# Two-layer trunk: causal mask by a bf16 product, softmax scaling on ScalarE, modulation chunks turned through DRAM

## The chip, the cores and the metric

The kernel runs on one core of a Trainium2 chip as one program. The metric is the time of one execution on the device in microseconds (us), median over runs. TensorE (PE in the rows) multiplies; VectorE (DVE), ScalarE (ACT) and GpSimd (POOL) work element by element; SyncE (SP) issues most of the DMAs. Each engine runs its own list of instructions in order and waits on semaphores for the others.

## The reference

512 tokens of width 1024 go through two layers. The conditioning vector c gives each layer six modulation vectors, which the kernel works out in three chunks of two (ada_w is 24 MB a layer). Layer 0 mixes tokens with 16-head attention with a forget gate, layer 1 with causal pooling; each layer ends in a mixture of 32 experts, two per token.

```
c_act = silu(c)
mod = c_act @ ada_w[i] + ada_b[i]
sh_m, sc_m, gt_m, sh_f, sc_f, gt_f = split(mod, 6)
h = rmsnorm(x, norm_mix_g[i]) * (1 + sc_m) + sh_m
# layer 0: attention, 16 heads of 64
logits = q @ k.T / 8 + F[t] - F[s]       # F = cumsum(log_sigmoid(x @ w_f + f_bias))
logits = where(s <= t, logits, -inf)
o = softmax(logits) @ v
x = x + gt_m * (o @ w_o)
h = rmsnorm(x, norm_ffn_g[i]) * (1 + sc_f) + sh_f
x = x + gt_f * experts(h)                # sigmoid router, best group of four, top 2 of 32
```

## The kernel before

**Attention.** The heads are taken in eight pairs (hp), each in four blocks of 128 queries (qt): 32 units, u = 4 hp + qt. `attention` writes the order of TensorE, VectorE and ScalarE by hand. A unit u does `flip(u)` (TensorE turns the scaled probabilities sb by products with the identity, L873; ScalarE copies them to pT, L874), then `scores(u + 1)`, then `normalise(u + 1)`, then `values(u)` (L882). `scores` makes 128 x n logits for each of the two heads in two products (L854 with the high parts of q and k, L855 with the low parts and the rows of the gate F); VectorE adds the causal mask on the last 128 columns (L856) and takes the negated maximum (L857); ScalarE takes the exponential with its sum (L858). `normalise` takes the reciprocal (L863) and multiplies the row by it on VectorE (L865).

**Projections.** Between these stand the steps of `project(hp + 1)`: 24 triples of products of 128x512 (L735) for q, k and v of the next pair. Numbers are split into a high and a low part of reduced precision, so each product is three. `close("q")` and `close("k")` take a finished sum out of PSUM: four casts on ScalarE (L771, L772 for q, L774, L775 for k) and two subtractions on VectorE (L778 for q, L781 for k). The v sum is turned by L789 and copied by VectorE (L791). `split` makes the halves of a pair's weights, the high one on ScalarE (L744), the low one on GpSimd (L745).

**Modulation.** Chunk (0, 0) is needed first: `ada_first` makes it on TensorE from eight loaded pieces. The other five chunks, 40 pieces in the list `late`, are multiplied and added up on VectorE, one piece of 128x2048 an operation (`ada_piece`, L332 and L334); the table `units` says after which unit each piece comes, EARLY pieces come before the loop. After the eighth piece TensorE sums over partitions (L342), `ada_turn` copies the row out of PSUM (L308), turns it into columns by 32 small products (L313), and `ada_close` adds the bias on VectorE (L350). The weights of everything come through one stream of slots in a fixed order. `small_loads` issues the small inputs, among them wf, the weights of the forget gates (used by `forget_gates`, L705).

**Behind the attention.** `wo_split` and `o_split` make the halves of the output weights and of the attention's result (ScalarE L919, VectorE L920); `out_ahead` and `out_step` multiply them. The router follows (L430 to L439), then the experts, whose large weight buffer can only be filled when the front's pools are closed.

## Time and profile before

| | us |
|---|---|
| median of 3 runs | 1364.91 |
| lowest and highest | 1362.5 and 1366.27 |
| the profiled execution | 1366.04 |
| its span in the trace | 1364.5 |
| mean granted TensorE clock | 0.946 |

The span is the time from the first to the last instruction of the trace; the profiled execution took 1.5 us more. In the rows below, times are microseconds from the start of the span unless marked ns. The granted clock is a share of 2.4 GHz: 0.50 is the lower of TensorE's two levels, 1.2 GHz. "[0.30 <-DVE sb L865]" says that the engine was idle for 0.30 us before the instruction and that line 865 on VectorE released it.

### The profile page before, as it was taken

The page shows a single profiled execution, that of the slowest core. Times are in us where ns is not written, and L with a number is a line of the kernel's source. Part 1 is how long each engine was busy: PE and PEld are TensorE (multiplying, and loading weights), DVE is VectorE, ACT ScalarE, POOL GpSimd, SP SyncE. Part 2 cuts the span into 40 slices and gives each one's busy share as a digit, 9 for nine tenths or more (in the row PEclk, how much of TensorE's full clock was granted, in tenths as well). Part 3 has the DMA queues.
Part 4 walks back from the last instruction along what each step waited for, and adds up shares of the span by engine and source line. Part 5 has one row for each costly group of instructions (what it writes and reads, how often), then busy time and mean ns, then how long its engine had stood idle before and what let it go on. Part 6 is the DMA issues. An engine that isn't in the chain of part 4 may idle for free.

```text
span 1364.5 us, 18527 instructions
## 1 busy us (share of the span) xinstructions
PE 1225.6 (90%) x6872; PEld 643.0 (47%) x6873; DVE 649.1 (48%) x1284; ACT 378.1 (28%) x754; POOL 127.9 (9%) x90
## 2 busy tenths in 40 slices
PE   5779999998899999998998977899999998998965
PEld 2557777766644444443443323644444443443322
DVE  2877877797643344332442334843334332442414
ACT  3545555643621111111111013721111111111013
POOL 1403333325200000000000010100000000000000
PEclk9889999979899999998999988999999998999987
DMA  9754755648489999999999999669999999999995
GB/s 364 239 186 140 271 181 197 253 168 312 162 340 419 418 420 420 422 427 422 427 426 426 419 413 406 256 242 416 417 420 420 422 426 423 427 426 427 426 412 212
DMA packets 77620, 479.26 MB, mean 351 GB/s; under 512 B 10982, under 2 KB 24422, under 8 KB 36276
## 3 DMA queue, kind: packets, MB, share of 16 engines
q1 hardware_dynamic: 76408, 475.33, 86.1%
q10 hardware_dynamic: 488, 1.80, 0.4%
q8 instruction: 57, 0.93, 0.3%
q0 software_dynamic: 624, 0.84, 0.2%
q14 instruction: 43, 0.35, 0.1%
HBM read 475.55 MB, written 2.38 MB: 350 GB/s over the span
## 4 chain that ended last, share of the span: by engine, by line
PE 63%; DVE 14%; DMA 13%; ACT 6%; issue 3%; SPq 0%; ACTq 0%; DVEq 0%
PE h L1187 23%; PE y L1218 11%; DMA w_more<-in_exp_w_dram 8%; PE h L735 6%; PE c L623 5%; DMA w<-in_exp_w_dram 3%; DVE lo L334 3%; PE t L1235 2%; PE t L1236 2%; DVE y L1208 1%; DVE yl L1179 1%; PE c L1236 1%; PE y L1227 1%; ACT yh L1178 1%; DVE mx L857 1%
## 5 line engine op out<-in xcount | busy, mean ns | idle before, releaser
L1187 PE MATMUL h<-w_more,xgT 128*32 128x512 f32 (+2 forms) x1040 | 304.0, 608 | 10.5 <-DMA w_more<-in_exp_w_dram 10.4
L1187 PE MATMUL h<-w,xgT 128*32 128x512 f32 (+2 forms) x944 | 300.8, 604 | 2.1 <-DMA w<-in_exp_w_dram 1.5
L1218 PE MATMUL y<-w_more,gT 128*32 128x512 f32 (+1 forms) x536 | 153.4, 644 | 14.0 <-DMA w_more<-in_exp_w_dram 10.2
L1187 PEld LDWEIGHTS h<-w_more,xgT 128*32 128x32 f32 (+2 forms) x1040 | 86.8, 125 | 120.6 <-issue 104.0
L1187 PEld LDWEIGHTS h<-w,xgT 128*32 128x32 f32 (+2 forms) x944 | 83.6, 124 | 100.5 <-issue 93.5
L1237 DVE TENSOR_TENSOR xs<-xs,t 128x512 f32<-128x512 f32 x100 | 64.1, 681 | 133.1 <-PE t L1236 133.0
L1218 PE MATMUL y<-w,gT 128*64 128x512 f32 (+2 forms) x280 | 110.0, 644 | 11.3 <-DMA w<-in_exp_w_dram 9.9
L1208 DVE SCALAR_TENSOR_TENSOR y<-y,gs,gt 128x512 f32<-128x512 f32 x52 | 39.2, 755 | 147.2 <-PE y L1218 135.4
L745 POOL TENSOR_TENSOR wl<-w,wh 128x1024 fp32r<-128x1024 f32 x32 | 88.9, 2784 | 192.5 <-ACT wh L744 190.2
L1195 DVE TENSOR_TENSOR yl<-yl,h 128x512 f32<-128x512 f32 x26 | 17.9, 688 | 185.4 <-PE h L1187 173.3
L1178 ACT CAST yh<-y 128x512 fp32r<-128x512 f32 x52 | 30.5, 587 | 253.6 <-DVE y L1208 253.6
L1117 ACT ACTIVATE xgT<-t,modT 128x128 f32<-128x128 f32 x104 | 46.0, 458 | 187.7 <-PE t L1139 185.4
L1187 PE MATMUL h<-w_side,xgT 128*32 128x512 f32 (+1 forms) x256 | 96.0, 595 | 0.0
L1218 PEld LDWEIGHTS y<-w_more,gT 128*32 128x32 f32 (+1 forms) x536 | 42.8, 129 | 80.3 <-issue 59.4
L1218 PE MATMUL y<-w_side,gT 128*64 128x512 f32 (+2 forms) x176 | 72.1, 621 | 1.2 <-DVE gT L1203 1.0
L735 PE MATMUL h<-hi,wh 128*128 128x512 f32 x168 | 72.0, 428 | 0.0
L334 DVE SCALAR_TENSOR_TENSOR lo<-w,cc,lo 128x2048 f32<-128x2048 f32 x28 | 71.6, 2557 | 0.4
L735 PE MATMUL h<-lo,wh 128*128 128x512 f32 x168 | 68.2, 406 | 0.0
L735 PE MATMUL h<-hi,wl 128*128 128x512 f32 x168 | 67.9, 404 | 0.0
L1193 ACT ACTIVATE yl<-h 128x512 f32<-128x512 f32 x26 | 15.6, 599 | 183.9 <-PE h L1187 183.9
L623 PE MATMUL c<-x,P 128*128 128x512 f32 x192 | 58.6, 427 | 8.4 <-DVE P L1150 8.4
L1218 PEld LDWEIGHTS y<-w,gT 128*64 128x64 f32 (+2 forms) x280 | 29.0, 133 | 47.2 <-issue 32.0
(373 smaller groups left out, 2047.5 us busy)
## 6 DMA issues: line engine op xcount, KB each, us to landing
w_more<-in_exp_w_dram SPq DMA_DIRECT2D x48, 2048.0 KB, 23.5
w_more<-in_exp_w_dram SPq DMA_DIRECT2D x87, 1024.0 KB, 14.6
w<-in_exp_w_dram SPq DMA_DIRECT2D x72, 1024.0 KB, 17.7
w<-in_exp_w_dram SPq DMA_DIRECT2D x35, 2048.0 KB
w<-in_ada_w_dram SPq DMA_DIRECT2D x48, 1024.0 KB, 5.1
w_side<-in_exp_w_dram SPq DMA_DIRECT2D x37, 1024.0 KB, 19.8
w_side<-in_exp_w_dram SPq DMA_DIRECT2D x11, 2048.0 KB
w<-in_attn_w_in_dram SPq DMA_DIRECT2D x12, 1024.0 KB, 8.0
```

Source lines behind the costliest of these rows:

```text
L334: V.scalar_tensor_tensor(ada_sum["s"], w, cc[:, j:j + 1], ada_sum["s"], op0=OP.mult, op1=OP.add)
L623: PE.matmul(pc[hf], P[part][:, t], R[("hi", "lo")[part]][:, t, 4 * hf:4 * hf + 4, :].rearrange("p j d -> p (j d)"), start=t == 0 and part ...
L735: PE.matmul(ps, a, b, start=first and n == 0, stop=last and n == 2)
L745: G.tensor_sub(lo, w, hi.bitcast(F32))
L1117: S.activation(xT[:, j, :], ps, AF.Identity, scale=A, bias=sh)
L1178: S.copy(yh, y)
L1187: PE.matmul(ps[r, :], xT[:, j, r], wt(name, ab, j, None), start=j == 0, stop=j == 7)
L1208: V.scalar_tensor_tensor(py, py, gs, R["gt"][:, 512 * hf:512 * hf + 512], op0=OP.mult, op1=OP.mult)
L1218: PE.matmul(py[hf][r, :], gT[:, j, r], wt("w2", ab, j, hf), start=j == 0, stop=j == 3)
L1235: PE.matmul(ps, PT[:, t, :], y[0], start=True, stop=False)
L1236: PE.matmul(ps, PT[:, t, :], y[1], start=False, stop=True)
L1237: V.tensor_add(xs[:, t, hs], xs[:, t, hs], ps)
```

## The change

1. The mask becomes a bf16 tile, and a third product with a bf16 identity (L864 after the change) adds it into PSUM; VectorE's addition L856 goes.
2. `normalise` multiplies by the reciprocal on ScalarE (L873 after the change) in place of VectorE.
3. Chunks other than (0, 0) are turned by two DMAs of GpSimd, out to DRAM and back into modT; `ada_close` comes one step of the generator later, with the bias added in place.
4. EARLY is 2 in place of 4; the pieces that stood in `project(0, True)` move into the loop, and the table doubles up from unit 26 in place of 28. One "x" more stands in ORDER0 (the hand-written order of the first expert stage).
5. The small loads are issued after pieces 1, 4 and 7 of `ada_first`, with wf in the second group; four steps of project(1) move ahead of the first normalisation, and units 0 to 3 take one step less each.

```diff
--- before.py
+++ after.py
@@ -46,12 +46,12 @@
 SIDE_SLOTS = 3
 MORE_SLOTS = 8
 WB = 4
-EARLY = 4
+EARLY = 2
 SPLITS = (2, 2)
 
 
 ORDER0 = (
-    "q03 w00 x w10 w01 c0 d0 v3 q0 w11 x r0 n0 U00 c1 U10 k00 w02 d1 h0 k10 q1 o0 r1 sigm L00 U01 L10 U11 "
+    "q03 w00 x w10 w01 c0 d0 v3 q0 w11 x r0 n0 U00 c1 U10 k00 w02 d1 h0 k10 q1 o0 r1 sigm x L00 U01 L10 U11 "
     "p0 k01 w12 k11 n1 s0 L01 g0 L11 c2 w03 p1 h1 d2 q2 l1 U02 s1 U12 k02 g1 w13 A0 k12 root A1 A2 A3 r2 "
     "A4 A5 A6 n2 A7 L02 h2 c3 L12 A8 d3 p2 A9 l2 U03 q13 s2 U13 r3 k03 g2 k13 sigm L03 n3 L13 A10 A11 A15 "
     "p3 A12 A16 A13 s3 A17 A14 g3 A18 A19 B0 A20 B1 A21 B2 B3 A22 B4 A24 B5 A25 y00 B6 A23 h3 B7 y10 A26 "
@@ -221,7 +221,7 @@
     units[30].append(("wo", 1, 0))
     units[31].append(("wo", 1, 1))
     for n, key in enumerate(late[EARLY:]):
-        units[min(n, 14 + n // 2)].append(("ada",) + key)
+        units[min(n, 13 + n // 2)].append(("ada",) + key)
 
     for j in range(8):
         ada_item(0, 0, j)
@@ -296,9 +296,9 @@
                 PE.matmul(ps[32 * g:32 * g + 32, :], crep[:, j, :], w[:, 512 * g:512 * g + 512],
                           start=j == 0, stop=j == 7)
             stream.done(("ada", 0, 0, j))
-            if j == 7 - FRONT_SLOTS:
-                small_loads(0)
-        small_loads(1)
+            if j in (1, 4):
+                small_loads(j // 4)
+        small_loads(2)
         for _ in ada_turn(0, 0, ps):
             pass
 
@@ -307,16 +307,22 @@
         row = front.tile([128, 512], F32, name="row", tag="row")
         S.copy(row, ps)
         yield
-        pm = bank("c")
-        for i in range(8):
-            for hf in range(2):
-                PE.matmul(pm[64 * hf:64 * hf + 64, 2 * i:2 * i + 2], row[:, i::8],
-                          ident[:, 32 * hf::64], start=True, stop=True)
-        ada_close(l, ch, pm[:, :16].rearrange("p (j v) -> p v j", v=2))
+        if (l, ch) == (0, 0):
+            pm = bank("c")
+            for i in range(8):
+                for hf in range(2):
+                    PE.matmul(pm[64 * hf:64 * hf + 64, 2 * i:2 * i + 2], row[:, i::8],
+                              ident[:, 32 * hf::64], start=True, stop=True)
+            ada_close(l, ch, pm[:, :16].rearrange("p (j v) -> p v j", v=2))
+            return
+        md = dram.tile([2 * D], F32, name=f"md{l}{ch}")
+        nc.gpsimd.dma_start(md.rearrange("(g n) -> g n", g=4), row[0:128:32, :])
+        pm = modT[l][:, 2 * ch:2 * ch + 2, :]
+        nc.gpsimd.dma_start(pm, md.rearrange("(v p j) -> p v j", v=2, j=8))
+        yield
+        ada_close(l, ch, pm)
         if (l, ch) == (1, 0):
-            md = dram.tile([D], F32, name="md")
-            nc.gpsimd.dma_start(md.rearrange("(g n) -> g n", g=2), row[0:64:32, :])
-            nc.gpsimd.dma_start(modC, md.rearrange("(c p) -> p c", c=8))
+            nc.gpsimd.dma_start(modC, md[:D].rearrange("(c p) -> p c", c=8))
             G.tensor_add(modC, modC, adabC)
             ma = dram.tile([D], F32, name="ma")
             nc.gpsimd.dma_start(ma.rearrange("(p j) -> p j", j=8), modT[1][:, 1, :])
@@ -650,6 +656,7 @@
         if k == 1:
             q.dma_start(wf[:, :, :H], attn_w_in[0, :, 3 * D:3 * D + H].rearrange("(p j) n -> p j n", j=8))
             q.dma_start(fb[:H], attn_f_bias[0][:, None])
+        if k == 2:
             bias(0, 2, 6)
             bias(1, 0, 6)
             q.dma_start(gains[:, 1, 0, :], norm_mix_g[1].rearrange("(p j) -> p j", j=8))
@@ -660,10 +667,13 @@
             q.dma_start(rw, router_w.rearrange("(p j) e -> p j e", j=8))
             q.dma_start(rbias, raw(router_bias, 0, [[0, 128], [1, NE]]))
 
-    cmask = front.tile([128, 128], F32, name="cmask")
+    cmask = front.tile([128, 128], BF16, name="cmask")
     V.memset(cmask, 0.0)
     G.affine_select(cmask, cmask, pattern=[[-1, 128]], compare_op=OP.is_ge, fill=NEG, base=0,
                     channel_multiplier=1)
+
+    ident_b = front.tile([128, 128], BF16, name="ident_b")
+    V.tensor_copy(ident_b, ident)
 
     def at(tag, shape, dt=F32, bufs=1):
         return att.tile([128] + shape, dt, name=tag, tag=tag, bufs=bufs)
@@ -815,10 +825,8 @@
             close("k", acc[1][1])
             for k in range(3):
                 terms(2, k)
-            steps(ada_piece(*late[2]), 1)
             split(1, "k")
             yield from close_v(acc[2][1])
-            steps(ada_piece(*late[3]), 1)
             return
         if hp > 1:
             bias_rows()
@@ -852,8 +860,8 @@
         for h in range(2):
             ps = bank("y")
             PE.matmul(ps[:, :n], stk[:, h, 0, q], stk[:, h, 1, :n], start=True, stop=False)
-            PE.matmul(ps[:, :n], b2[:68, h, 0, q], b2[:68, h, 1, :n], start=False, stop=True)
-            V.tensor_tensor(ps[:, n - 128:n], ps[:, n - 128:n], cmask, OP.add)
+            PE.matmul(ps[:, :n], b2[:68, h, 0, q], b2[:68, h, 1, :n], start=False, stop=False)
+            PE.matmul(ps[:, n - 128:n], ident_b, cmask, start=False, stop=True)
             V.tensor_reduce(mx[:, h:h + 1], ps[:, :n], AX.X, OP.max, negate=True)
             S.activation(sb[:, h, :n], ps[:, :n], AF.Exp, bias=mx[:, h:h + 1], accum_out=ls[:, h:h + 1])
         return sb, ls
@@ -862,7 +870,7 @@
         n = 128 * (u % NT + 1)
         V.reciprocal(ls, ls)
         for h in range(2):
-            V.tensor_scalar(sb[:, h, :n], sb[:, h, :n], ls[:, h:h + 1], None, op0=OP.mult)
+            S.activation(sb[:, h, :n], sb[:, h, :n], AF.Copy, scale=ls[:, h:h + 1])
 
     def flip(u, sb):
         qt = u % NT
@@ -941,6 +949,7 @@
         steps(gen, 8)
         steps(first, 1)
         sb, ls = scores(0)
+        steps(gen, 4)
         normalise(0, sb, ls)
         split(1, "v")
         for u in range(32):
@@ -959,7 +968,7 @@
                 steps(old, 1)
             if u < 31:
                 normalise(u + 1, sb, ls)
-            steps(gen, 4 - 2 * (qt == 0) if hp else 2)
+            steps(gen, 4 - 2 * (qt == 0) if hp else 1)
             if 25 <= u < 29:
                 wo_split(0, u - 25)
             for j in {28: (2, 3), 29: (5, 6)}.get(u, ()):
```

The lines behind the change are shifted: L857 becomes L865, L858 L866, L863 L871, L865 L873, L873 L881, L771 L781, L772 L782, L774 L784, L778 L788, L781 L791, L334 L340, L920 L928.

On ScalarE, in units 9 and 10 (the q close of head pair 3), before the change:

```order
L858 ACTIVATE sb,ls<-y,mx 128x384 x2
L771 ACTIVATE stk<-h 64x512
L772 ACTIVATE b_1067<-h 64x512
L771 ACTIVATE stk<-h 64x512
L772 ACTIVATE b_1067<-h 64x512
L874 COPY pT<-t 128x384 x2
L858 ACTIVATE sb,ls<-y,mx 128x512 x2
L774 CAST stk<-h 64x512
L775 CAST stk<-h 64x512
```

and after it:

```order
L866 ACTIVATE sb,ls<-y,mx 128x384 x2
L873 ACTIVATE sb<-sb,ls 128x384 x2
L781 ACTIVATE stk<-h 64x512
L782 ACTIVATE b_1048<-h 64x512
L781 ACTIVATE stk<-h 64x512
L782 ACTIVATE b_1048<-h 64x512
L882 COPY pT<-t 128x384 x2
L866 ACTIVATE sb,ls<-y,mx 128x512 x2
L873 ACTIVATE sb<-sb,ls 128x512 x2
L784 CAST stk<-h 64x512
L785 CAST stk<-h 64x512
```

The pair of passes L873 stands between the exponentials and the four q casts; in the next unit another pair stands ahead of the k casts.

On VectorE, ahead of the loop and in its first two units, before the change (the first L334 is late[2], the second late[3]):

```order
L781 TENSOR_TENSOR b_308<-h,stk 64x512 x2
L334 SCALAR_TENSOR_TENSOR lo<-w,cc,lo 128x2048
L778 SCALAR_TENSOR_TENSOR stk<-h,stk 64x512 x2
L791 COPY vs<-t 128x512
L334 SCALAR_TENSOR_TENSOR lo<-w,cc,lo 128x2048
L856 TENSOR_TENSOR y<-y,cmask 128x128
L857 TENSOR_REDUCE mx<-y 128x1
L856 TENSOR_TENSOR y<-y,cmask 128x128
L857 TENSOR_REDUCE mx<-y 128x1
L863 RECIPROCAL ls<-ls 128x2
L865 TENSOR_SCALAR sb<-sb,ls 128x128 x2
```

and after it:

```order
L791 TENSOR_TENSOR b_310<-h,stk 64x512 x2
L788 SCALAR_TENSOR_TENSOR stk<-h,stk 64x512 x2
L801 COPY vs<-t 128x512
L865 TENSOR_REDUCE mx<-y 128x1 x2
L871 RECIPROCAL ls<-ls 128x2
L865 TENSOR_REDUCE mx<-y 128x1 x2
L871 RECIPROCAL ls<-ls 128x2
L340 SCALAR_TENSOR_TENSOR lo<-w,cc,lo 128x2048
L865 TENSOR_REDUCE mx<-y 128x1 x2
L871 RECIPROCAL ls<-ls 128x2
L791 TENSOR_TENSOR b_312<-h,stk 64x512 x2
L340 SCALAR_TENSOR_TENSOR lo<-w,cc,lo 128x2048
```

The two ada pieces ahead of the first maximum are gone: one L340 stands behind the second reciprocal, and the next behind the k close.

On VectorE, from the q close of the last pair to the first o_split, before the change:

```order
L781 TENSOR_TENSOR b_2149<-h,stk 64x512 x2
L334 SCALAR_TENSOR_TENSOR lo<-w,cc,lo 128x2048
L856 TENSOR_TENSOR y<-y,cmask 128x128
L857 TENSOR_REDUCE mx<-y 128x1
L856 TENSOR_TENSOR y<-y,cmask 128x128
L857 TENSOR_REDUCE mx<-y 128x1
L863 RECIPROCAL ls<-ls 128x2
L865 TENSOR_SCALAR sb<-sb,ls 128x128 x2
L334 SCALAR_TENSOR_TENSOR lo<-w,cc,lo 128x2048
L920 TENSOR_TENSOR lo_305<-x,hi_304 128x4x128 x2
```

and after it:

```order
L791 TENSOR_TENSOR b_2096<-h,stk 64x512 x2
L340 SCALAR_TENSOR_TENSOR lo<-w,cc,lo 128x2048 x2
L865 TENSOR_REDUCE mx<-y 128x1 x2
L871 RECIPROCAL ls<-ls 128x2
L340 SCALAR_TENSOR_TENSOR lo<-w,cc,lo 128x2048 x2
L928 TENSOR_TENSOR lo_307<-x,hi_306 128x4x128 x2
L865 TENSOR_REDUCE mx<-y 128x1 x2
```

Where one ada piece stood behind a unit's normalisation or k close there are two, ahead of the first o_split L928.

## Rows read from the trace of the kernel before

**Rows 1.** Busy times by stage: stretch, its us, engines' busy us (instructions), clock, DMA
```profile
0.00:80.40 80.40, 49.23 (x251) 29.77 (x252) 48.32 (x80) 35.10 (x59) 21.08 (x27) 0.89 0.78 283
80.40:105.10 24.70, 23.00 (x124) 17.17 (x125) 18.16 (x35) 12.10 (x31) 4.77 (x2) 0.87 0.57 189
105.10:262.00 156.90, 152.73 (x947) 119.48 (x947) 123.90 (x209) 91.57 (x208) 53.11 (x24) 0.98 0.60 209
262.00:310.70 48.70, 43.77 (x233) 33.30 (x232) 42.21 (x57) 21.39 (x48) 11.32 (x4) 0.82 0.54 195
310.70:328.70 18.00, 12.20 (x67) 9.27 (x65) 17.20 (x9) 6.28 (x8) 10.34 (x3) 1.00 0.62 209
328.70:364.00 35.30, 34.49 (x214) 26.74 (x214) 15.14 (x35) 16.83 (x26) 14.68 (x10) 0.90 0.46 193
364.00:1364.50 1000.50, 910.19 (x5040) 407.25 (x5040) 384.21 (x866) 194.81 (x377) 12.64 (x20) 0.95 0.96 399
```

**Rows 2.** The same for two pairs of heads, and two half-clock stretches
```profile
134.12:161.76 27.64, 26.02 (x153) 20.17 (x152) 22.96 (x38) 16.25 (x37) 8.72 (x3) 1.00 0.86 294
161.76:192.09 30.33, 30.05 (x193) 23.67 (x192) 22.63 (x40) 16.94 (x38) 8.80 (x4) 0.94 0.34 118
175.40:178.90 3.50, 3.50 (x13) 2.92 (x12) 2.81 (x4) 0.49 (x2) 0.57 (x1) 0.51 0.04 8
271.00:277.80 6.80, 6.63 (x21) 5.48 (x22) 5.56 (x4) 3.36 (x6) 2.37 (x1) 0.50 0.19 51
```

**Rows 3.** Timeline ahead of the first flip: start, us, engine, line [idle before]
```profile
73.74 1.39 DVE L778 SCALAR_TENSOR_TENSOR stk<-h,stk 64x512 fp32r<-64x512 f32 x2 [3.38 <-ACT b L772]
...
75.88 2.35 DVE L334 SCALAR_TENSOR_TENSOR lo<-w,cc,lo 128x2048 f32<-128x2048 f32 x1
...
80.37 0.73 PE L873 MATMUL t<-ident,sb 128*128 128x128 f32 x2 [8.15 <-DVE sb L865]
```

**Rows 4.** Timeline: the forget gates' product, the first q close, the next q projection
```profile
48.28 2.84 PE L705 MATMUL c<-x,wf 128*32 128x512 f32 x16 [4.42 <-DMA wf<-in_attn_w_in_dram]
...
61.22 1.39 DVE L778 SCALAR_TENSOR_TENSOR stk<-h,stk 64x512 fp32r<-64x512 f32 x2 [0.24 <-ACT b L772]
...
65.78 0.39 PE L735 MATMUL h<-hi,wh 128*128 128x512 f32 x1
```

**Rows 5.** Timeline of units 9 to 11, ScalarE, VectorE, then TensorE
```profile
143.54 0.58 ACT L771 ACTIVATE stk<-h 64x512 fp32r<-64x512 f32 x1
...
145.84 1.39 DVE L778 SCALAR_TENSOR_TENSOR stk<-h,stk 64x512 fp32r<-64x512 f32 x2 [0.77 <-ACT b L772]
...
147.27 2.35 DVE L334 SCALAR_TENSOR_TENSOR lo<-w,cc,lo 128x2048 f32<-128x2048 f32 x1
...
153.29 1.06 PE L873 MATMUL t<-ident,sb 128*128 128x128 f32 x8 [0.30 <-DVE sb L865]
```

**Rows 6.** Timeline of the boundary from unit 11 to 12
```profile
152.32 0.56 ACT L774 CAST stk<-h 64x512 fp32r<-64x512 f32 x1
...
155.45 0.33 PE L855 MATMUL y<-b 68*128 68x128 f32 x1 [1.03 <-DVE b L781]
```

**Rows 7.** Groups by line, 72 to 320 us (count | busy, mean ns), and one on the chain
```profile
L856 DVE TENSOR_TENSOR y<-y,cmask 128x128 f32<-128x128 f32 x64 | 18.7, 291 | 8.3 <-PE y L855 8.0
...
L919 ACT CAST hi<-x 128x512 fp32r<-128x512 f32 x8 | 4.7, 619 | 0.0
...
L865 DVE TENSOR_SCALAR sb<-sb,ls 128x512 f32<-128x512 f32 x16 | 7.1, 484 | 0.3
...
173.26 1.81 PE c L313 x32
```

**Rows 8.** One DMA issue of GpSimd, L362, issue to landing
```profile
DMA to landing us min/median/max: 1.7/1.7/2.6
```

**Rows 9.** Timeline of the tail, VectorE and TensorE
```profile
273.84 4.07 DVE L334 SCALAR_TENSOR_TENSOR lo<-w,cc,lo 128x2048 f32<-128x2048 f32 x1
...
285.38 0.80 PE L735 MATMUL h<-wh,lo 128*128 128x512 f32 x1 [2.23 <-DVE lo L920]
```


## Prediction

> **What bounds the kernel now.** I read the busy times by stage first [rows 1]. The span falls into a head (to the first flip, 80.4 us), eight pairs of heads with four units each (80.4 to 310.7), 53 us of output projection and router, and 1,000 us of experts in which the DMA engines are busy 0.96 of the time. The first expert weights for the big buffer are issued only when the front's pools close at 364, so I count every microsecond that the front gains or loses as one of the whole. None of the edits touches the experts. Then I asked what the front waits for. In the steady stretch from 105.1 to 262.0 TensorE is busy 152.7 of 156.9 us while VectorE has 123.9 and ScalarE 91.6 [rows 1]. That reads as "TensorE is the bound". The timeline says something finer: from unit 9 to unit 11 there is a chain through ScalarE and VectorE that is exactly as long as TensorE's work. After the exponentials ScalarE makes the four q casts from 143.54; VectorE's q close waits for them until 145.84; behind it stands an ada piece of 2.35 us at 147.27; behind that the maximum of the next unit, its exponential, its normalisation; and the flip at 153.29 waits 0.30 us for it [rows 5]. At the boundary the same again: the k casts start at 152.32, the k close follows them, and TensorE waits 1.03 us for it [rows 6]. So a step put into this chain costs time although TensorE looks full.
>
> **Head and first pair.** Ahead of the first flip TensorE sits idle 8.15 us; on VectorE the time goes to the q close (73.74 to 75.13), the copy of the values, an ada piece of 2.35 us, and the masks [rows 3]. The order of VectorE in front of this section shows that this piece is gone from there, and so are the masks (0.29 each [rows 7]). That is 2.35 + 0.1 to 0.3. Besides, wf is issued after the fifth of the eight pieces of ada_first instead of after the eighth: TensorE waited 4.42 us for it [rows 4]. Not all of that comes through, since the next q projection needs a bank that VectorE frees only at 61.22 + 1.39 = 62.6; it started at 65.78 [rows 4], so 3.1 us is what it can gain. So the first flip comes 3.1 + 2.4 = 5.5 us earlier; the twelve product matmuls that now stand before it fill its wait and are hidden by it. The four units of the first pair give perhaps 0.8 more, as the last ada piece there moves behind the k close (0 to 2). Sum: -6.3; if wf is still late, -3.
>
> **Steady pairs.** The normalisation leaves VectorE, where a 512-wide one took 0.48 us [rows 7], and comes to ScalarE, which runs nothing out of its order. No ScalarE pass of that shape exists in this trace. The nearest row is the 128x512 cast, 0.62 us [rows 7]; I take 0.6 for 512 columns and 0.5 for 384, and as bounds 0.48 (VectorE's) and 0.75. The order of ScalarE shows two of them between the exponentials and the four q casts. In units 9 to 11: the maxima come about 0.3 us earlier without the masks; then the two passes take 2 x 0.5, and 0.2 to 0.3 goes to the reciprocal's round trip, so the casts start 1.0 to 1.3 later, and with them the q close, the ada piece, the maximum, the exponential and the flip: +1.06. At the boundary the k casts started 0.97 us before the flip (152.32 against 153.29 [rows 5, 6]); now they come behind the second pass, about 0.6 us after the flip may start: +1.6 to +1.7, all of it TensorE's wait, because the next scores need the k close. So a pair whose chain is tight grows by 2.8. Such is the pair from 134.12 to 161.76 (27.64 us). The next one, 161.76 to 192.09, takes 30.33 us and TensorE is busy 30.05 of them [rows 2]: it carries the turning of an ada chunk (L313, 1.81 us [rows 7]) and then 3.5 us at a clock of 0.51 [rows 2], which costs 1.7. These two go away, yet its chain is at least that of its neighbour, 27.64 + 2.8 = 30.4, so that it gains nothing: +0.1 to +1.3, I take +0.45. From 105.1 to 262 there are three pairs of the first kind and two and a half of the second: 3 x 2.8 + 2.5 x 0.45 = +9.5. VectorE's relief, 18.7 us of masks [rows 7] and all of the normalising, is real but is not in this sum, since VectorE waits for ScalarE where it matters. The masks on TensorE are 64 small products with their weight loads; the flip of 128x128 in 1.06/8 = 0.13 us each [rows 5] is the nearest row, the whole 0.33 us of L855 [rows 6] the upper bound. They lie in the time in which TensorE waits for the chain; were that cover gone, 64 x 0.13 = 8 us (0 to 21).
>
> The Trainium skill ("ScalarE: Activation LUTs", section "What ACT_TABLE_LOAD costs") gives an ACTIVATE with a per-partition operand 280 ns and 0.833 ns a column, 0.71 us for 512, against 0.62 in the row. By the page each pair would pay about 0.2 us more in its two closes, 1 us in all; the row is of a cast without such an operand, so no run here shows it yet.
>
> **Turning through DRAM.** Each later chunk is now written out and read back by GpSimd, and the close waits for it. An issue of that kind lands in 1.7 to 2.6 us [rows 8]; two are 3.4 to 5.2, while the close comes a unit later (about 7 us) and GpSimd is busy 53.1 of 156.9 us [rows 1]. I cost it at nothing; if the close waited after all, VectorE would stand for up to 2 us, three times in this stretch: +6.
>
> **Tail.** From 262.0 to 310.7 VectorE is the tight one, 42.2 of 48.7 us [rows 1]. The ada pieces that left the head come back here: its order shows two in one place in units 26 and 27 and the o_split L928 behind them, where before there was one. TensorE waited 2.23 us for that very L920 already [rows 9]. A piece takes 2.35 us [rows 3], but 4.07 while GpSimd subtracts [rows 9]. Two at 4.1 less the masks and passes that VectorE no longer has in these units (2 x 1.1) is +6. Bounds: 0, where the relief of the later units gives it back, and +8.
>
> **Last flip to router, and the output projection.** 18.0 us with VectorE busy 17.2 [rows 1]; the last normalisation (2 x 0.48) and contention fall away: -1.5 (0 to -3). In 328.7 to 364 one more L313 (1.81) goes, and with it a half-clock stretch like that of 3.5 us: -3.5 (-2 to -4).
>
> **Sum.** -6.3 + 9.5 + 6 - 1.5 - 3.5 = +4.2. The clock: after TensorE's idle time at 271 it ran at 0.50 for 6.8 us [rows 2], and longer waits at the boundaries will bring some of this: +1.5. In all +5.7 on 1366.0, the profiled run's own time (span 1364.5 and 1.5 around it), which is 1371.7; the median of the runs shown is 1.1 lower, so 1370.5 is what I put against it. 0.3% (4.1 us) is about what a measurement of this kernel can tell: 1360.8 to 1369.0 is "the same".
>
> **Rivals.** (a) *ScalarE's order does not bind* (chance 0.2; ends faster). VectorE is freed of the masks and the passes, so its ada pieces and the next maxima start earlier, ScalarE gets its scores earlier, and the passes lie where ScalarE now waits for the maxima. For it: the second kind of pair has almost no wait now. Against it: the q close waited 0.77 us for ScalarE already [rows 5]. The first kind of pair then grows by 0.7 only, the tail by 2, and the clock costs nothing: -6.3 + 2 + 2 - 5 = -7.3, 1357.6. It decides when the casts start less than 0.4 us later after the flip than now. (b) *Half of it is hidden* (0.25; same): +6 in the pairs, +4 in the tail, +1 of clock, 1364.7. (c) *The clock falls at every boundary* (0.15; slower): TensorE waits 1.0 + 0.3 there now and keeps the clock at 1.00 in the pair from 134.12 [rows 2]; at 3 us it may lose it as at 271, and seven falls of about 1 to 1.7 us bring 1378. [...]
>
> **Chances.** The forecast, 1369 to 1375 alone, has 0.4. So faster 0.2, same 0.25, slower 0.55. 8 in 10 takes in (a) and nearly all of (c): 1357 to 1378.
>
> **What would show it.** The first flip at about 75 and the fifth at 98.7 (head right). ScalarE's q casts some 5 us after the flip of their unit and TensorE's wait at the first scores of a pair near 3 us (chain right); if those waits stay near 1, (a) holds. L928 later and TensorE's idle time before it longer (tail right). No L313 but one group. A VectorE wait on a DMA at the close would show the DRAM turn on the path. The prediction is wrong as a whole if the pairs become shorter than 27.6 us: then VectorE, not ScalarE, was what TensorE waited for.

## The result, and the profile after

The changed kernel takes 1380.06 us (median of 4, 1377.12 to 1381.27) against 1365.55 for the kernel before beside it (the three runs of the table above and a fourth): ratio 1.0103, 95% interval 1.0087 to 1.0119. It is slower, as forecast, but by 14.5 us where 5.7 were forecast, and just outside the range of 1357 to 1378. The profiled span is 1378.6 us, 14.1 longer. The stages of the changed kernel, in the columns of [rows 1]; the cuts are the fifth, the 27th and the last flip, the router's first product (L445) and the first issue for the big expert buffer:

```profile
0.00:102.42 102.42, 74.64 (x385) 48.45 (x387) 56.19 (x93) 51.32 (x99) 25.90 (x29) 0.88 0.72 252
102.42:272.86 170.44, 160.39 (x895) 118.33 (x894) 97.67 (x119) 109.07 (x251) 50.97 (x29) 0.94 0.56 190
272.86:327.82 54.96, 41.60 (x211) 28.89 (x209) 40.92 (x39) 25.94 (x59) 12.33 (x7) 0.88 0.58 201
327.82:342.96 15.14, 12.43 (x67) 9.34 (x67) 15.03 (x9) 6.43 (x9) 8.19 (x3) 1.00 0.91 332
342.96:377.37 34.41, 31.04 (x182) 23.51 (x182) 14.36 (x36) 17.43 (x27) 17.53 (x13) 0.95 0.44 176
377.37:1378.60 1001.23, 911.81 (x5040) 408.57 (x5040) 384.20 (x866) 194.40 (x377) 12.72 (x20) 0.95 0.96 398
```

Against the same cuts before (105.11, 262.02, 310.73, 328.75, 364.07) the head and first pair are 2.7 us shorter, the steady pairs 13.5 longer (170.4 against 156.9), the tail 6.2 longer (55.0 against 48.7), the stretch to the router 2.9 shorter, the output projection 0.9 shorter and the experts 0.8 longer: +14.1 in all. VectorE's busy time in the steady stretch fell from 123.9 to 97.7 us, and the stretch grew all the same. TensorE, which was busy 0.97 of it, is now busy 0.94 of a longer one, at a clock of 0.94 in place of 0.98.

Most of the loss sits in one place, the boundary of two pairs, from the flip of a pair's last unit to the flip of the next pair's first. The five boundaries of the steady stretch take 10.94, 11.58, 10.83, 12.68 and 10.95 us, where they took 7.26, 8.47, 7.28, 8.47 and 7.26: +18.2 us. All other units of the stretch together are 4.7 us shorter. Here is the boundary from unit 11 to 12 in windows, from the flip to the first projection step and from there to the next flip, first before the change:

```profile
153.29:156.34 3.05, 1.73 (x13) 1.45 (x13) 1.81 (x4) 2.99 (x6) 0.00 (x0) 1.00 0.54 221
156.34:161.76 5.42, 5.42 (x35) 4.16 (x36) 4.76 (x9) 1.89 (x6) 3.94 (x1) 1.00 0.44 130
```

and after it:

```profile
153.62:158.14 4.52, 2.32 (x14) 1.61 (x15) 1.61 (x3) 4.45 (x8) 0.00 (x0) 1.00 0.18 74
158.14:165.20 7.06, 7.06 (x36) 5.37 (x36) 5.81 (x5) 2.44 (x8) 3.94 (x1) 0.76 0.44 151
```

The first window grew by 1.5 us: TensorE's idle time in it went from 1.32 to 2.20 us, and the rest is mostly a flip of 1.27 in place of 1.06 us and the mask's products. The second grew by 1.6 us with the same products in it, at a clock of 0.76 in place of 1.00. What TensorE waits for shows in the timeline of the changed kernel, ScalarE, VectorE and TensorE:

```profile
152.85 1.33 ACT L873 ACTIVATE sb<-sb,ls 128x512 f32<-128x512 f32 x2 [0.23 <-DVE ls L871]
...
154.09 0.56 ACT L784 CAST stk<-h 64x512 fp32r<-64x512 f32 x1
...
156.47 1.41 DVE L791 TENSOR_TENSOR b<-h,stk 64x512 fp32r<-64x512 f32 x2 [3.66 <-ACT stk L785]
...
153.62 1.27 PE L881 MATMUL t<-ident,sb 128*128 128x128 f32 x8 [0.21 <-ACT sb L873]
...
157.21 0.33 PE L863 MATMUL y<-b 68*128 68x128 f32 x1 [1.59 <-DVE b L791]
...
158.51 0.63 PE L745 MATMUL h<-hi,wl 128*128 128x512 f32 x1
```

The two passes L873 (ScalarE's multiplications by the reciprocal) take 1.33 us and the first k cast follows at 154.09; the k close on VectorE starts at 156.47 and TensorE waits 1.59 us for it. The next projection products then take 0.63 us in the row where their neighbours at full clock take 0.39.

### The profile page after: what moved, and what is told of

Its sections match the earlier page's. It is cut to its first block, busy times and chain, and to the rows that moved or that the text cites. A ratio compares the mean times of both kernels' runs of the same rounds, so it can differ in the third digit from the quotient of the medians.

```text
span 1378.6 us, 18302 instructions
## 1 busy us (share of the span) xinstructions
PE 1231.9 (89%) x6776; PEld 637.1 (46%) x6777; DVE 608.4 (44%) x1157; ACT 404.6 (29%) x818; POOL 127.6 (9%) x99
## 4 chain that ended last, share of the span: by engine, by line
PE 58%; DVE 14%; DMA 13%; ACT 10%; issue 3%; POOL 1%; SPq 0%; ACTq 0%; DVEq 0%; POOLq 0%
PE h L1196 23%; PE y L1227 10%; DMA w_more<-in_exp_w_dram 8%; PE h L745 6%; PE c L629 5%; DMA w<-in_exp_w_dram 3%; DVE lo L340 2%; PE t L1244 2%; ACT sb L866 2%; PE t L1245 2%; DVE y L1217 2%; DVE yl L1188 1%; PE c L1245 1%; PE y L1236 1%; ACT sb L873 1%
## 5 line engine op out<-in xcount | busy, mean ns | idle before, releaser
L1227 PE MATMUL y<-w_more,gT 128*32 128x512 f32 (+1 forms) x536 | 152.0, 630 | 13.7 <-DMA w_more<-in_exp_w_dram 9.8
L755 POOL TENSOR_TENSOR wl<-w,wh 128x1024 fp32r<-128x1024 f32 x32 | 83.6, 2617 | 173.8 <-ACT wh L754 159.5
L340 DVE SCALAR_TENSOR_TENSOR lo<-w,cc,lo 128x2048 f32<-128x2048 f32 x28 | 80.8, 2886 | 0.4
L745 PE MATMUL h<-hi,wh 128*128 128x512 f32 x168 | 77.9, 463 | 3.1 <-DVE stk L788 3.1
L745 PE MATMUL h<-hi,wl 128*128 128x512 f32 x168 | 71.2, 424 | 0.0
L745 PE MATMUL h<-lo,wh 128*128 128x512 f32 x168 | 71.0, 423 | 0.0
L629 PE MATMUL c<-lo,P 128*128 128x512 f16 x192 | 51.1, 389 | 1.4 <-issue 1.4
```

Of the source, the lines that this page charges most:

```text
L340: V.scalar_tensor_tensor(ada_sum["s"], w, cc[:, j:j + 1], ada_sum["s"], op0=OP.mult, op1=OP.add)
L629: PE.matmul(pc[hf], P[part][:, t], R[("hi", "lo")[part]][:, t, 4 * hf:4 * hf + 4, :].rearrange("p j d -> p (j d)"), start=t == 0 and part ...
L745: PE.matmul(ps, a, b, start=first and n == 0, stop=last and n == 2)
L755: G.tensor_sub(lo, w, hi.bitcast(F32))
L1227: PE.matmul(py[hf][r, :], gT[:, j, r], wt("w2", ab, j, hf), start=j == 0, stop=j == 3)
```

## The experiments

All times are medians; ratios are to the kernel before on the same chip, with 95% intervals. The median of the kernel before lies between 1365.5 and 1367.2 us from chip to chip, and an interval reaches 1.5 to 5 us to either side, so a difference of 2 or 3 us between two of the kernels means little by itself.

**The passes on ScalarE alone.** The edit in the kernel before:

```diff
-            V.tensor_scalar(sb[:, h, :n], sb[:, h, :n], ls[:, h:h + 1], None, op0=OP.mult)
+            S.activation(sb[:, h, :n], sb[:, h, :n], AF.Copy, scale=ls[:, h:h + 1])
```

> The kernel before with one edit alone: the multiplication by the reciprocal goes to ScalarE. Theory 1 (at the boundary of two pairs the two ScalarE passes stand ahead of the k casts, TensorE waits about 1.5 us longer for the k close, and the clock then falls for about 3.3 us, 1.6 us more): seven boundaries at 3.1 us, some 1380 to 1390, with half clock behind each boundary. Rival (the passes fill time in which ScalarE waits; the loss comes from the ada pieces moved, the masks on TensorE or the turn through DRAM): within 4 us of 1365.5.

1390.05 us, ratio 1.0161 (1.0142 to 1.0181), the upper end of theory 1. With the masks still on VectorE it is worse than the whole change. Its boundary from unit 11 to 12:

```profile
158.48 1.27 PE L873 MATMUL t<-ident,sb 128*128 128x128 f32 x8 [1.54 <-ACT sb L865]
...
160.15 0.33 PE L854 MATMUL y<-stk 128*128 128x128 f32 x1 [0.40 <-ACT stk L775]
...
162.06 0.47 PE L855 MATMUL y<-b 68*128 68x128 f32 x1 [1.59 <-DVE b L781]
...
170.81 0.38 PE L873 MATMUL t<-ident,sb 128*128 128x128 f32 x2
```

It takes 12.33 us, flip to flip, with the same waits of 0.40 and 1.59 us as in the changed kernel and one more of 1.54 at the flip. The rival falls.

**The passes back on VectorE, the rest of the change kept.** The same line the other way round.

> The changed kernel with that one edit undone, everything else kept. Theory 1: the waits at the boundaries go back to about 1.3 us, the clock stays at 1.00, and 7 x 3.1 us come back: 1355 to 1363. Rival: at most 5 us come back, 1375 or more.

1353.67 us, ratio 0.9899 (0.9878 to 0.9919): 26 us come back, more than the forecast allowed, and the rest of the change is worth 13.5. The boundary of unit 11 in the same two windows:

```profile
147.95:149.96 2.01, 1.80 (x16) 1.54 (x14) 1.61 (x3) 1.62 (x4) 0.00 (x0) 1.00 0.01 4
149.96:155.41 5.45, 5.45 (x37) 4.20 (x37) 4.71 (x7) 2.09 (x6) 3.58 (x1) 1.00 0.43 155
```

2.0 us to the first step, less than the 3.05 of the kernel before, because the two masks of 0.29 us [rows 7] no longer stand before the k close and the maxima (the run with the mask alone, below, has 1.99 us here); and no fall of the clock.

**Work put into the wait.** Four steps of the projection move ahead of the first scores of a pair:

```diff
+            if qt == 3 and hp:
+                steps(gen, 4)
             if u < 31:
                 sb, ls = scores(u + 1)
...
-            steps(gen, 4 - 2 * (qt == 0) if hp else 1)
+            steps(gen, (4, 4, 4, 0)[qt] - 2 * (qt == 0) if hp else 1)
```

> The changed kernel with the four projection steps (12 products, 2.8 us) that TensorE has behind the first scores of a new pair moved ahead of them, from pair 1 on; the k close and its wait are not touched. Theory 1: the wait of some 4.5 us at each of six boundaries shrinks by 2.8 us and the clock is kept, 1.6 us more: 6 x 4.4 = 26 us, about 1352 to 1358. Rival (the passes make the chain longer in every unit, and the boundary is only where it shows): the wait turns up at the next flip, at most 5 us come back.

1366.98 us, ratio 0.9999 (0.9988 to 1.0011), 13 us less than the changed kernel: half of what theory 1 asked. TensorE's rows at unit 11:

```profile
149.84 1.27 PE L881 MATMUL t<-ident,sb 128*128 128x128 f32 x8 [0.23 <-ACT sb L873]
...
153.69 0.22 PE L862 MATMUL y<-stk 128*128 128x128 f32 x1
...
158.33 0.62 PE L881 MATMUL t<-ident,sb 128*128 128x128 f32 x2 [1.17 <-ACT sb L873]
```

The scores find the k close done, but the flip of unit 12 waits 1.17 us, as its maxima and passes come behind. So the wait was partly moved, which the rival said, though its 5 us were far passed: the boundaries went from 10.94 to 6.80 and from 11.58 to 8.49, 19.6 us over the five. What is missing from theory 1 lies mostly behind them: the sixth boundary, from unit 27 to 28, kept its 12.6 us, and the tail grew by 3.2 us (58.2 against 55.0).

**Work that nobody reads, in the same wait.** Twelve products ahead of the first scores, overwritten by them:

```diff
+            if u % NT == 0 and 4 < u and h == 0:
+                for _ in range(12):
+                    PE.matmul(ps, hi0[:, 0, 0, :], by_slice(hi0, 0), start=True, stop=True)
```

> The changed kernel with twelve products of 128x512 added ahead of the first scores of each new pair from pair 2 on; nobody reads their result, so the chain is as long as before and TensorE has 2.8 us more work in the time in which it waited. Theory 1, its clock part by itself: no half clock behind the boundaries, 6 x 1.6 = 10 us less, about 1370. Rival (the clock falls for another reason, or its fall is hidden): 1380, or more by the added products.

1372.72 us, ratio 1.0040 (1.0026 to 1.0055). The two windows:

```profile
154.31:158.84 4.53, 4.53 (x26) 3.75 (x27) 1.60 (x3) 4.46 (x8) 0.00 (x0) 1.00 0.16 67
158.84:164.29 5.45, 5.45 (x36) 4.20 (x36) 4.74 (x5) 2.31 (x8) 3.94 (x1) 1.00 0.44 156
```

The first is as long as in the changed kernel (4.53 against 4.52), so the chain is untouched (at three of the other boundaries it is 0.1 to 0.25 longer). The second is 5.45 in place of 7.06, at clock 1.00. All five boundaries of the steady stretch keep the clock at 1.00 in both windows and give back 8.2 us; the sixth, from unit 27 to 28, gives nothing (12.59 and 12.61). The clock part is shown by itself.

**The other parts, each alone in the kernel before.** The edits are those of the change's diff: its item 1 (the mask on TensorE), its item 3 with the "x" (the turn through DRAM), and the rest of items 4 and 5 (the loads, EARLY and the table, the four steps ahead of the first normalisation).

> The kernel before with the mask alone moved to TensorE. The parts other than the passes together gave 13.5 us; this asks for the mask's share. Theory: the products are short and partly hidden, VectorE loses 18.7 us of which only what stands in the chain counts, so between -3 and +3 of the kernel before. Rival (VectorE's relief is what shortened the waits at the boundaries): -6 or more.

1363.18 us, ratio 0.9989 (0.9966 to 1.0011): no difference that shows in the time. In its trace the tight boundary of unit 11 takes 7.41 us in place of 8.47, and the tail 42.6 in place of 48.7; the steady stretch is 2.9 us longer all the same. Units 5 and 6 have 2.1 of it, at a clock of 0.90 behind the first turned chunk in place of 1.00; and units in which TensorE does not wait pay for the products: 8 and 9 go from 5.88 and 6.06 to 6.13 and 6.33, some 0.13 us for each of their two products.

> The kernel before with the turning through DRAM alone (and the one step more in the expert stage's order that finishes the last chunk). Theory: the pairs with L313 lose its 1.8 us and the half clock behind it, and become as short as their neighbours: from 30.3 to about 27.7 us, 2.5 times, and 1 to 3 us in the tail and in the output projection: -8 to -11. Rival (the close waits for the two DMAs on VectorE): 0 or slower.

1358.10 us, ratio 0.9949 (0.9932 to 0.9966), 7.7 us less, just short of the forecast. The units behind a turned chunk shorten as expected (8.74 to 6.08 us at unit 13), but the boundaries behind them grow from 7.3 to 8.5: their first window goes from 1.8 to 3.05 us, that of unit 11, so the chain of the k close, hidden until then by L313, ends last there too.

> The kernel before with the earlier small loads, EARLY 2 with its table, and the four steps ahead of the first normalisation. Theory: the first flip some 4 us earlier, as in the changed kernel, and the tail 2 to 4 us longer by the two pieces more in units 26 and 27: -2 (-4 to +1). Rival (the tail gives nothing back): -5.

1367.45 us, ratio 1.0018 (1.0002 to 1.0033). The first flip comes at 75.66, 4.7 us earlier, the fifth 3.9 us, and the tail takes 2.4 us of this back (51.1 us against 48.7). The median is 1.7 us above the kernel before, over the forecast; the profiled execution was the fastest of ten, 1.8 us under the median, so its trace does not show where the rest went.

The three parts alone sum to some -8.6 us, together they gave -13.5; the difference is about as large as the uncertainty of the four ratios together. The traces say that part of it is real: the first windows of the boundaries take 3.05 us with the turn alone, 1.9 to 2.0 with the mask alone and 1.4 to 2.0 with all three, so the mask takes away the wait that the turn's removal lays bare. No run has these two alone.

**The table of the ada pieces.** In the kernel with the passes on VectorE two pieces are put into earlier units, so that doubling begins at unit 28 again; the two numbers choose the units (9 and 17 give units 9 and 16):

```diff
-        units[min(n, 13 + n // 2)].append(("ada",) + key)
+        n -= (n > 9) + (n > 17)
+        units[min(n, 14 + n // 2)].append(("ada",) + key)
```

> The changed kernel with the normalisation back on VectorE and the table altered: two extra ada pieces in units 9 and 16, and doubling from unit 28 again in place of 26. Theory (in this kernel TensorE bounds the steady units and has no wait there, so an extra piece is free, and the pieces of units 26 and 27 are what lengthens the tail): 3 to 5 us less than with the table of the change, 1349 to 1351. Rival (VectorE is as full in the steady units, or the tail is long for another reason): the same 1353.7 or more.

1353.92 us, ratio 0.9921 (0.9892 to 0.9951), no gain over 1353.67, the rival's time. The tail became 7.4 us shorter (44.1 against 51.5), and the steady units lost 8.3: the boundaries behind units 11 and 19 went from 7.5 to 10.1 us, the clock behind the first of them at 0.76. Unit 9 is the one with the q close.

Units 12 and 20, with 12 and 21 in the table:

> The changed kernel with the normalisation on VectorE and the two extra ada pieces in units 12 and 20, the first units of a pair, in place of 9 and 16; doubling from unit 28. Theory: an extra piece is free where VectorE closes neither q nor k; so the steady units stay as with the table of the change and the tail is 7 us shorter, as with the pieces in units 9 and 16: 1345 to 1349. Rival (VectorE has no room for a piece in any steady unit): 1352 to 1356, with longer pairs behind units 12 and 20.

1346.26 us, ratio 0.9855 (0.9821 to 0.9889). In this kernel and in the one with both edits below, the sum of chunk (1, 0) is taken from a tile that the first piece of chunk (1, 1) has replaced; the amount of work is the same, but the modulation that comes out is not the reference's.

The same with the four moved steps of above:

> Both of the two before: the normalisation on VectorE, the extra pieces in units 12 and 20, the four steps moved. Theory: the two add up at most, 1343 to 1349; where an extra piece makes the k close later, the moved steps cover it. Rival (the maxima of the next pair come later behind the moved steps and the tail loses what is gained): not under 1350.

1344.64 us, ratio 0.9837 (0.9802 to 0.9872).

The moved steps without the extra pieces:

> The changed kernel with the normalisation on VectorE and the four steps moved ahead of the first scores of a pair. Theory 1: the wait there is only some 0.7 us in this kernel and the clock is kept already, so there is little to fill: 1349 to 1355. Rival (the order of the steps gives time by itself, whatever the wait): as much as it gave with the passes on ScalarE, 13 us, 1341.

1350.31 us, ratio 0.9884 (0.9850 to 0.9918), where the boundaries that took 7.5 us take 6.8; as theory 1 said, hardly a gain, and none that the intervals show.

Units 12 and 24, with 12 and 25 in the table:

> As the run with extra pieces in units 12 and 20, but in units 12 and 24, so that no chunk begins in the unit in which the one before it ends; the output is the reference's here. Theory: the steady units keep their times, the tail loses 6 to 9 us against the table of the change: 1344 to 1349. Rival (the gain of that run came from the sum of chunk (1, 0) being taken early from another tile): 1352 or more.

1350.86 us, ratio 0.9901 (0.9878 to 0.9924), between theory and rival: unit 28 is 5.1 us shorter, but the extra piece of unit 24 holds up the flips of units 26 and 27, which wait 1.03 and 2.72 us.

The same with the four moved steps:

> The same with the four steps ahead of the first scores of each pair. Theory: 1 to 4 us less again, 1341 to 1347, and the tail as in the run without them. Rival: no less than without the moved steps.

1350.96 us, ratio 0.9895 (0.9877 to 0.9914): nothing more, as the rival said.

Units 12 and 16, with 12 and 17 in the table:

> The extra ada pieces in units 12 and 16, every chunk's sum kept. Theory (the pieces of units 26 and 27 lengthen the tail, and in units 12 and 24 the second of the two was too near the tail and held up the flips of units 26 and 27): the steady units as with the table of the change, units 26 to 28 some 8 us shorter, 1344 to 1348. Rival (the tail's gain needs the chunk's wrong sum): 1350 or more.

1349.09 us, ratio 0.9877 (0.9854 to 0.9900), above the forecast. The tail is 44.1 us against 51.5; 2 us are lost again at units 18 and 19. The 1346.26 of units 12 and 20 is not reached with every sum kept and the steps in their old place, so how much of it came from the sum taken early stays open.

The same with the four moved steps:

> The same with the four steps ahead of the first scores of each pair. Theory: 0 to 3 us less than without, 1342 to 1347. Rival: nothing, as in units 12 and 24.

1344.56 us, ratio 0.9839 (0.9818 to 0.9859), 4.5 us less than without the moved steps, where 0 to 3 were forecast: 22 us less than the kernel before and some 35 less than the changed one. It is the fastest kernel here that keeps every chunk's sum.

**The passes where nothing waits behind them.** ScalarE keeps those of the first two units of a pair, VectorE takes the others:

```diff
+            if u % NT < 2:
+                S.activation(sb[:, h, :n], sb[:, h, :n], AF.Copy, scale=ls[:, h:h + 1])
+            else:
+                V.tensor_scalar(sb[:, h, :n], sb[:, h, :n], ls[:, h:h + 1], None, op0=OP.mult)
```

> The changed kernel with the passes of the third and fourth unit of each pair back on VectorE (those ahead of the q and the k casts), the others on ScalarE. Theory 1 (a pass costs time only where casts that others wait for stand behind it): all of the 26 us come back, 1352 to 1356. Rival (each pass on ScalarE costs its share, about half of the columns-and-overhead time is still there): 1362 to 1368.

1354.90 us, ratio 0.9919 (0.9891 to 0.9946), the time of the kernel with all passes on VectorE. So the passes that stay on ScalarE cost nothing that shows; the ones that cost are those of the third and fourth units, ahead of the q and k casts. These are also the wide ones (609 and 715 ns against 394 and 502), so this run does not part place from width, nor the q casts from the k casts; the boundary's rows above show the passes of the fourth unit at work.

## Why the prediction was wrong

**The step that failed is the clock's, priced at +1.5.** The longer wait itself was nearly right. At the boundaries that the prediction worked out, from unit 11 to 12 and from 19 to 20, the first window grew by 1.47 and 1.62 us, where it said "+1.6 to +1.7, all of it TensorE's wait"; at unit 11 0.88 us of this is idle time of TensorE, and the wait at the first scores alone is 1.59 us against 1.03, not the 3 of the sign. The fall of the clock behind such a wait was rival (c), chance 0.15, and it was the case, behind all five steady boundaries: 1.6 us at unit 11 and 8.2 us over the five, as the unread products show. The second windows of the other four:

```profile
126.76:133.80 7.04, 7.04 (x36) 5.21 (x36) 4.74 (x5) 2.91 (x8) 3.09 (x2) 0.76 0.71 229
189.73:196.50 6.77, 6.77 (x36) 5.15 (x36) 4.58 (x5) 2.75 (x8) 3.10 (x2) 0.79 0.73 235
221.02:229.03 8.01, 8.01 (x37) 5.92 (x36) 5.66 (x5) 2.27 (x8) 3.95 (x1) 0.65 0.49 149
253.35:260.38 7.03, 7.03 (x37) 5.33 (x36) 6.32 (x5) 2.92 (x8) 4.26 (x4) 0.76 0.60 175
```

Of the 8.4 us between +5.7 and +14.1, the steady stretch holds 2.5 (13.5 against 9.5 and the clock's 1.5), the head and first pair 3.6, the output projection 2.6, the experts 0.8 and the tail 0.2; the stretch to the router gives 1.4 back. The clock is the largest single miss, 6.7 us at the five boundaries, and part of it is hidden by the next one.

**Steady pairs, +9.5 against +13.5.** Without the clock's 8.2 us some 5.3 are left where +9.5 stood. So this term was too large. Its count of pairs was the wrong way round: L313 stands at 116.74, 173.09 and 231.06, so three pairs are of the second kind (the first of them without half clock behind L313, 29.01 us) and two and a half of the first, and the prediction's own prices give +8.4. The +1.06 from unit 9 to 11 was too much: 13.29 became 13.69, and with the passes alone 14.54. The prediction counted 0.3 us for the masks here; the rest of the change gave 0.85 back, so VectorE's relief, which "is not in this sum", should have been in it in part. The casts give the sign that was asked for: those of q in unit 9 start 4.4 us after its flip in place of 3.5, where rival (a) wanted less than 0.4 more. A pass of 512 columns took 0.715 us, where I took 0.6; the mask's product is 0.245 in its row, overlapped with its neighbours, and cost 0.13 us where TensorE did not wait, as priced:

```profile
L873 ACT ACTIVATE sb<-sb,ls 128x512 f32<-128x512 f32 x16 | 10.7, 715 | 1.9 <-DVE ls L871 1.9
...
L864 PE MATMUL y<-cmask,ident_b 128*128 128x128 bf16 x62 | 15.2, 245 | 0.0
```

The cast's row, without a per-partition operand, was the wrong neighbour. The Trainium skill ("ScalarE: Activation LUTs", section "What ACT_TABLE_LOAD costs") gives an ACTIVATE with one per-partition operand 280 ns and 0.833 ns a column; the estimate from it for 512 columns, 0.71 us, agrees with this trace's 0.715.

**Head and first pair, -6.3 against -2.7.** The load and the missing ada piece did what was said: the projection starts at 63.05 against 62.6 forecast. But TensorE had waited 3.08 us there and ran its first products at half clock (0.50 up to 66.0); and the flip at 95.20 waits 3.65 us for a chain through the passes, the k casts, the k close, an ada piece, the next maxima and their passes, with a clock of 0.64 up to the fifth flip:

```profile
63.05 0.76 PE L745 MATMUL h<-hi,wh 128*128 128x512 f32 x1 [3.08 <-DVE stk L788]
...
64.03 0.63 PE L745 MATMUL h<-lo,wh 128*128 128x512 f32 x1
...
88.20 1.41 DVE L791 TENSOR_TENSOR b<-h,stk 64x512 fp32r<-64x512 f32 x2 [3.43 <-ACT stk L785]
...
89.64 2.35 DVE L340 SCALAR_TENSOR_TENSOR lo<-w,cc,lo 128x2048 f32<-128x2048 f32 x1
...
95.20 1.12 PE L881 MATMUL t<-ident,sb 128*128 128x128 f32 x4 [3.65 <-ACT sb L873]
```

The same flip with the passes on VectorE and the same ada pieces:

```profile
93.32 1.94 PE L881 MATMUL t<-ident,sb 128*128 128x128 f32 x8 [2.64 <-DVE sb L873]
```

The unit before it takes 7.74 us there, 9.26 in the changed kernel and 7.65 before, so most of its loss is the passes' and not the piece's. The prediction gave the first flip at about 75 (it came at 76.46) and gained 0.8 in the first pair, which lost 1.2.

**Tail, +6 against +6.2.** The place was right, the size in part by luck. Two ada pieces take 6.45 and 6.71 us in units 26 and 27, and TensorE waits 3.58 us for L928:

```profile
286.26 6.45 DVE L340 SCALAR_TENSOR_TENSOR lo<-w,cc,lo 128x2048 f32<-128x2048 f32 x2
...
294.00 6.71 DVE L340 SCALAR_TENSOR_TENSOR lo<-w,cc,lo 128x2048 f32<-128x2048 f32 x2
...
300.63 1.28 DVE L928 TENSOR_TENSOR lo<-x,hi 128x512 fp32r<-128x512 f32 x2
...
301.36 0.80 PE L745 MATMUL h<-wh,lo 128*128 128x512 f32 x1 [3.58 <-DVE lo L928]
```

With those two pieces in units 12 and 16 (line numbers one higher), single pieces stand there and the wait is 2.00 us:

```profile
262.08 4.08 DVE L341 SCALAR_TENSOR_TENSOR lo<-w,cc,lo 128x2048 f32<-128x2048 f32 x1
...
267.95 2.35 DVE L341 SCALAR_TENSOR_TENSOR lo<-w,cc,lo 128x2048 f32<-128x2048 f32 x1
...
270.59 3.07 DVE L929 TENSOR_TENSOR lo<-x,hi 128x512 fp32r<-128x512 f32 x2 [0.29 <-ACT hi L928]
...
273.11 0.50 PE L746 MATMUL h<-wh,lo 128*128 128x512 f32 x1 [2.00 <-DVE lo L929]
```

Here the table shows as a cause: against the kernel with the passes on VectorE and the table of the change, 51.5 us of tail became 44.1 with nothing else changed. The passes are another, which the prediction had as relief: alone, without the extra pieces, they make the tail 53.1 us in place of 48.7, and the change with them has 3.4 us more than without.

**Last flip to router, -1.5 against -2.9; output projection, -3.5 against -0.9.** L313 went, but GpSimd, whose order is not written by hand, now makes its four additions L1012 before the last subtraction for the output weights; TensorE waits 2.19 us for it, and the clock of 350 to 356 is 0.75. The prediction did not look at GpSimd's order here. Before the change the subtraction stood behind the first addition:

```profile
329.32 1.27 POOL L1003 TENSOR_TENSOR xs<-xs,tmp 128x512 f32<-128x512 f32 x1 [1.57 <-DVE tmp L1002]
330.55 2.38 POOL L745 TENSOR_TENSOR wl<-w,wh 128x1024 fp32r<-128x1024 f32 x1
332.88 3.78 POOL L1003 TENSOR_TENSOR xs<-xs,tmp 128x512 f32<-128x512 f32 x3
```

and after it:

```profile
344.43 5.00 POOL L1012 TENSOR_TENSOR xs<-xs,tmp 128x512 f32<-128x512 f32 x4
...
349.38 2.35 POOL L755 TENSOR_TENSOR wl<-w,wh 128x1024 fp32r<-128x1024 f32 x1
...
351.79 0.50 PE L745 MATMUL y<-wl,hi 128*128 128x512 f32 x1 [2.19 <-POOL wl L755]
```

The four kernels with every pass on ScalarE have this order, the one with the passes alone among them (it too waits 2.19 us), and all others have the old one, that with the passes back on VectorE among them. So it comes with the passes. The stretch from the last flip to the router goes with it, 13.7 to 15.1 us against 18.0 to 18.2: the -2.9 there is not the relief of VectorE that the prediction had in mind.

**Turning through DRAM at nothing** was right, though the DMAs took longer than the 3.4 to 5.2 us of the prediction (1.7 to 5.4 us out and 2.9 to 5.1 back): no VectorE wait on a DMA appears, and alone the turn gains 7.7 us. Rival (a), that ScalarE's order does not bind, is refuted by the two runs that move the passes alone. Rival (b), the same time as before, fell as well.

## What to carry to other kernels

Before moving work to an idle engine, list what stands behind it in that engine's order and who waits for that: passes of 0.4 to 0.7 us on an engine busy 0.6 of the time cost some 26 us, and those with no cast behind them, the narrower half, cost nothing that shows. Price a longer wait of TensorE with the half clock that may follow it: over the five boundaries the first windows grew by 9.5 us and the second, at half clock for a part, by 8.8. And a wait that cannot be shortened can be filled with products that are due anyway.

## What the runs showed of the hardware

Twelve products that nobody reads, put into a wait, made the kernel about 7 us faster than without them, since TensorE kept its 2.4 GHz level behind the wait (granted clock 1.00 against 0.76 in the window after it). Before the change a wait of 1.03 us at the same place [rows 6], with one of 0.30 us ahead of it at the flip, had left the clock at 1.00. In the changed kernel the wait there is 1.59 us at all five boundaries, at two of them behind one of 0.40 us, and the clock fell behind all five. With the extra ada pieces in units 9 and 16 the wait behind unit 11 was again 1.03 us, but the flip ahead of it had waited 1.14 us, and the clock fell to 0.76:

```profile
149.74 1.06 PE L882 MATMUL t<-ident,sb 128*128 128x128 f32 x8 [1.14 <-DVE sb L874]
...
151.90 0.33 PE L864 MATMUL y<-b 68*128 68x128 f32 x1 [1.03 <-DVE b L792]
```
